# Weight sums in DRAM: copies issued by ScalarE, adds queued behind the decay rows, bias rows and last weights asked for earlier

## The chip, the cores and the metric

The kernel runs on one core of a Trainium2 chip. The core has five engines that run side by side, each through its own queue in order: TensorE (PE, matmuls; its weight loads are PEld), VectorE (DVE), ScalarE (ACT), GpSimd (POOL) and SyncE (SP). SP, ACT and POOL can issue DMAs, which 16 DMA engines carry out. The metric is the device time of one execution in microseconds. Before the change it is 1393.98 us, the median of three runs.

## What is computed

One decoder layer over 512 tokens of width 1024, in float32:

```
x = x + 0.5 * swiglu(rms_norm(x), ffn1_w_in, ffn1_w_out)          # D_FF = 2816
x = x + hybrid_mixer(rms_norm(x), ...)
x = x + memory_cross_attention(rms_norm(x), rms_norm(mem), ...)   # 256 memory tokens, 4 heads
x = x + 0.5 * swiglu(rms_norm(x), ffn2_w_in, ffn2_w_out)
return rms_norm(x)

# hybrid_mixer: one input projection, two groups of heads, one output projection
z, xbc, dt, q, k, v = split(h @ w_in)
y_ssd  = ssd_scan(conv(xbc), dt) * silu(z)      # 16 heads of 64, 4 groups, chunks of 128
#   decay = exp(la_cum[l] - la_cum[s]);  y = (c b^T * decay) xdt + carried state
y_attn = diff_attention(q, k, v, rel_bias)      # 8 heads, two softmaxes each
#   logits = q k^T / 8 + bias[bucket(k_pos - q_pos)]
return concat(y_ssd, y_attn) @ w_out
```

## The kernel before, in words

**Matmuls.** Each float32 weight tile is loaded to a buffer `wr` (six of them) and split into a high part `wh` by ScalarE (L151) and a low part `wl` by VectorE (L152), three buffers each. A product is three matmuls, high by high and the two mixed ones. `load_w` (L168) does load and split, `proj` (L296) a projection over eight tiles, 24 matmuls of 512 columns.

**Weight sums.** The last FFN multiplies in 2 by 2 blocks with seven products in place of eight (`quad`, L248, and `out_blocks`, L1107). Some of the seven take sums of weight blocks. These sums are made in DRAM while the mixer runs, by `block_sums_in_dram` (L1084): 46 jobs, each a copy of a block of 512 KB (a few of 256 KB) from the weights to `isum` or `wsum`, and an add, a DMA with accumulation of a second block onto it. Only POOL issues adds. Some add a sum that an earlier job made. The FFN's input sums are read by `quad`, its output sums by `out_blocks`; both start after the cross-attention.

**The order of the work.** The program is written as generators. `Order` (L53) runs them: the dense ones (projections) one after the other, and beside them chains (heads, groups, norms, the sums) that say after how many planned microseconds `od.t` they go on (`yield`). `od.t` counts matmul time alone. The instructions of SP stay in the order in which the program issues them; those of the other engines are set into their queues by a planner at build time, which may lift an instruction that it takes to be ready over an earlier one. `behind(ins)` (L180) forbids that against the instructions named: what is issued inside comes later in the same engine's queue. It adds an order, not a wait. `recent` holds the last weight tile's two split instructions. The list `hold` has an entry while a state-space group is between its start and its second set of decays; the sums then issue nothing.

**Attention heads.** `queries_keys(hd)` (L639) projects q, then k, and spawns `head(hd)` 3.4 planned us later. `head` first asks for the bias row of that head (L650, POOL, from the table `rel_z` in DRAM, 256 KB) and then makes scores (L653): a VectorE operation adds the bias and takes the minimum `mn` (L665), ScalarE takes exponentials, TensorE turns them (`turn`, tile `pt`).

**State-space groups.** `group(g)` (L779) runs four times. Its `decays(j)` (L785) asks POOL for two decay rows `r` (L790), 256 KB each, cumulated logs of one head broadcast to 128 partitions in pieces of 512 bytes. ScalarE makes exponentials of them (L849 to L852), VectorE multiplies by the masked products `cbm` (L853), and TensorE then makes `py` from them (L863). A group's norm uses POOL for a power (L335) and for one half of the row's diagonal (`ndiag`, L346).

**The end.** In `out_blocks` of the last third of the FFN, the product with `blocks[B22]` into `e_ps` is followed by `update` of two tiles, which calls `final`: squares on ScalarE, gain and scale on VectorE, a power on POOL (L1211), and two stores to the output by SP (L1213, L1215). Then follows the product with `sums[3]` into `b_ps`, whose weights are loaded by SP (L1117), and the last two updates with their stores.

Of the kernel before, what the change touches and what calls it, by code (L numbers as in the profile page):

```python
# [17 lines left out]
P = 128  # L18
# [11 lines left out]
RW = 640  # L30
NSLOT = 55
NHALF = 16

W = {"h0": 3.4, "hs": 3.3, "hv": 2.08, "hp": 6.75}
W |= {"g0": 8.28, "gc": 0.75, "gx": 0.92, "gb": 2.59, "gs": 0.51, "gd": 6.9, "gy": 0.38, "gq": 11.02, "gn": 6.52}
# [61 lines left out]
def body(tc, a, dbg=None):  # L97
# [13 lines left out]
    def nm(s):  # L111
        uid[0] += 1
        return f"{s}_{uid[0]}"
# [12 lines left out]
    def acc(s, shape=(P, T)):  # L126
        return acc_p.tile(list(shape), F32, tag="acc", name=nm(s))
# [5 lines left out]
        if dbg and name in dbg:  # L133
            nc.sync.dma_start(dbg[name], t.bitcast(F32) if t.dtype == R32 else t)

    last, start, last_sum, recent, hold = [], [], [], [], []
    V, S, G = nc.vector, nc.scalar, nc.gpsimd
    od = Order()

# [19 lines left out]
    def split(s, src, scale=None, half=False, n=T):  # L159
        if half:  # L160
            both = s2(s, R32, (P, 2, T // 2))
            hi, lo = both[:, 0], both[:, 1]
        else:
            hi, lo = s2(s + "h", R32, (P, n)), s2(s + "l", R32, (P, n))
        last[:] = [i.ins for i in split_into(hi, lo, src, scale)]
        return hi, lo
# [472 lines left out]
    def queries_keys(hd):  # L639
        pq = acc("pq")  # L640
        yield from proj(pq, load_w(a["wq"][hd]), h)
        q = split("q", pq, -1.0)
        pk = acc("pk")
        yield from proj(pk, load_w(a["wk"][hd]), h)
        kq = split("k", pk)
        od.spawn(head(hd, q, kq), W["h0"])

    def head(hd, q, kq):
        bias = s2("bias")
        nc.gpsimd.dma_start(bias, bass.AP(rel_z.tensor, rel_z.offset + hd * P * (RW + 1) + P - 1, [[RW, P], [1, T]]))  # L650
        es, w0, w1 = {}, {}, {}
        sm = [small("sm", 4) for _ in range(2)]

        def scores(i):
            n = P * (i + 1)
            ps = [aux("ps") for _ in range(2)]
            for j, (u, w) in enumerate(((0, 0), (0, 1), (1, 0))):
                for c in range(2):
                    pc = slice(64 * c, 64 * c + 64)
                    mm(ps[c][:, :n], q[u][pc, i * P : (i + 1) * P], kq[w][pc, :n], j == 0, j == 2)  # L660
            es[i] = []
            for c in range(2):
                ec = s2("ec", shape=(P, n))
                mn = small("mn", 1, bufs=8)
                V.tensor_tensor_reduce(out=ec[:, :n], in0=ps[c][:, :n], in1=bias[:, T - n :], scale=0.125, scalar=3e38, op0=ALU.add, op1=ALU.min, accum_out=mn)  # L665
                S.activation(ec[:, :n], ec[:, :n], AF.Exp, bias=mn, scale=-1.0, accum_out=sm[c][:, i : i + 1])  # L666
                es[i].append(ec)

        def combine(i):

            n = P * (i + 1)
            e = es[i]
            rc = small("rc", 1)
            V.reciprocal(rc, sm[1][:, i : i + 1])
            rl = small("rl", 1)
            V.scalar_tensor_tensor(rl, sm[0][:, i : i + 1], nlam, rc, ALU.mult, ALU.mult)
            V.scalar_tensor_tensor(e[0][:, :n], e[1][:, :n], rl, e[0][:, :n], ALU.mult, ALU.add)
            e.pop()

        def turn(j):  # L680
            n = P * (4 - j)
            pt = aux("pt")
            for i in range(j, 4):
                transpose(pt[:, (i - j) * P : (i - j + 1) * P], es[i][0][:, j * P : (j + 1) * P])
            if n <= T // 2:
                both = s2("wt", R32, (P, 2, n))
                w0[j], w1[j] = both[:, 0], both[:, 1]
            else:
                w0[j], w1[j] = s2("wt", R32, (P, n)), s2("wt", R32, (P, n))
            split_into(w0[j], w1[j], pt[:, :n])  # L690

        for s in range(6):
            if s < 4:
                scores(3 - s)
            if 1 <= s < 5:
                combine(4 - s)
            if s >= 2:
                turn(5 - s)
            yield W["hs"]
        es.clear()  # L700
        while hd // 4 not in vs:
            yield 1.0
        v = vs[hd // 4]
        hs = slice((hd % 4) * P, (hd % 4 + 1) * P)
        po = aux("po")
        for j in range(4):
            mm3(po[:, j * P :], v[j], (w0[j], w1[j]), j == 0, j == 3, wc=hs)
        w0.clear()
        w1.clear()
        of = s2("of")  # L710
        S.activation(of, po, AF.Copy)
        yield W["hv"]
        pt = aux("ptk")
        for b in range(4):
            transpose(pt[:, b * P : (b + 1) * P], of[:, b * P : (b + 1) * P])
        ss = small("ss", 4)
        junk = s2("junk", shape=(P, P))
        for b in range(4):
            S.activation(junk, pt[:, b * P : (b + 1) * P], AF.Square, accum_out=ss[:, b : b + 1])
        ev = small("ev", 4)  # L720
        V.scalar_tensor_tensor(ev, sm[0], EPS, sm[0], ALU.mult, ALU.mult)
        V.scalar_tensor_tensor(ev, ss, 1.0 / P, ev, ALU.mult, ALU.add)
        rr = small("rr", 4)
        G.tensor_tensor(rr, ev, mhalf, ALU.pow)
        on = s2("on", shape=(P, 4, P))
        V.tensor_tensor(on, pt.rearrange("p (a b) -> p a b", b=P), rr[:, :, None].to_broadcast([P, 4, P]), ALU.mult)
        yield W["hp"]
        pt = aux("pot")
        for b in range(4):
            transpose(pt[:, b * P : (b + 1) * P], on[:, b])  # L730
        ya[hd] = split("ya", pt, wsub)
        dump(f"ya_{hd}", ya[hd][0])
# [46 lines left out]
    def group(g, bt, ct, xs, zs):  # L779
# [5 lines left out]
        def decays(j):  # L785
            rs = []
            for hh in range(2):
                r = s2("r", shape=(P, 4, P))
                hd = 4 * g + 2 * j + hh
                nc.gpsimd.dma_start(r, bass.AP(cum_d.tensor, cum_d.offset + hd * P, [[0, P], [16 * P, 4], [1, P]]))  # L790
                rs.append(r)
            return rs

        hold.append(g)
# [289 lines left out]
    def block_sums_in_dram():  # L1084
        jobs = []
        for c, (f0, nf) in enumerate(THIRDS):
            gs = range(f0 // 2, (f0 + nf) // 2)
            jobs += [(isum[g][0], a["f2q"][g][0], a["f2q"][g][1]) for g in gs]
            jobs += [(isum[g][1], a["f2q"][g][2], isum[g][0]) for g in gs]
            blocks, sums = a[f"f2b{c}"], wsum[c]  # L1090
            for t, (to, more) in enumerate(((blocks[B12], blocks[B11]), (blocks[B12], blocks[B22]), (blocks[B22], sums[0]), (blocks[B21], sums[2]))):
                for k in range(0, nf // 2 * T, D):
                    ks = slice(k, min(k + D, nf // 2 * T))
                    jobs.append((sums[t][:, ks], to[:, ks], more[:, ks]))
        for n in range(len(jobs) + 2):
            while hold:
                yield 1.0
            if n < len(jobs):
                nc.sync.dma_start(jobs[n][0], jobs[n][1])
                yield 4.0  # L1100
            while hold:
                yield 1.0
            if n > 1:
                G.dma_start(jobs[n - 2][0], jobs[n - 2][2], accum_op=ALU.add, max_dma_last_dim=4 * D)
                yield 6.0

    def out_blocks(c, g, col4, last):  # L1107

# [2 lines left out]
        n = len(g)  # L1111
        parts = [(k, min(k + 2, n)) for k in range(0, n, 2)]

        def weights(of, part):
            w = (part[1] - part[0]) * T
            raw = wp.tile([P, w], F32, tag="wr", name=nm("wr"), bufs=6)
            nc.sync.dma_start(raw, of[:, part[0] * T : part[1] * T])  # L1117
            hi = wp.tile([P, w], R32, tag="wh", name=nm("wh"))
            lo = wp.tile([P, w], R32, tag="wl", name=nm("wl"))
            split_into(hi, lo, raw)  # L1120
            return hi, lo
# [8 lines left out]
                    nc.tensor.matmul(ps, a_[:, ts], b_[:, ws], start=first and k == 0 and j == 0, stop=k == n - 1 and j == 2, skip_group_check=True)  # L1130
                yield

        def product(ps, of, which, first=False, by_pair=False):
            if by_pair:
                ws = [weights(of, part) for part in parts]
                for t in range(2):
                    for w, part in zip(ws, parts):
                        yield from some(ps[t], w, which, part, t, first)
                return
            for part in parts:  # L1140
                w = weights(of, part)
                for t in range(2):
                    yield from some(ps[t], w, which, part, t, first)
# [36 lines left out]
        for t in range(2):  # L1180
            c22 = s2("c22")
            V.tensor_tensor(c22, p5[t], b_ps[t], ALU.subtract)
            update(t + 2, 1, c22)
        yield from product(e_ps, blocks[B22], S4)
        for t in range(2):
            update(t, 1, e_ps[t])
        yield from product(b_ps, sums[3], "22", by_pair=last is not None)
        for t in range(2):
            update(t + 2, 0, b_ps[t])

# [131 lines left out]
```

## Time and profile before

| What | Value |
|---|---|
| median of three runs | 1393.98 us (1392.22 to 1394.95) |
| the profiled execution: its own time, and its span | 1396.56 us, 1394.8 us |
| mean granted clock of TensorE | 0.98 |
| DMAs issued by SP: bytes, share of the DMA engines' time | 173.63 MB, 38.0% |
| DMAs issued by POOL | 47.79 MB, 20.7% |
| copies for sums: isum, wsum of 512 KB, issue to landing | 8.3 us, 5.5 us (medians) |
| adds for sums, issue to landing | 7.0 to 8.8 us (medians) |
| decay rows r; bias rows, issue to landing | 12.7 us; 6.0 us (medians) |

The profile is of one execution. Its span runs from the first to the last instruction; an engine is busy while it computes, and issuing a DMA isn't counted as busy for SP and ACT. A wait is put down to the instruction or DMA that ended it. A name such as `wsum<-in_f2b` gives what is written and what is read; L1104 is a line of the file. The granted clock is 1.00 at full speed; in this profile its records are either 1.0 or 0.5, so a mean between them says what part of a stretch ran at half speed. A time of "issue to landing" runs from the issuing instruction to the end of the transfer.

### The profile page before, as it was taken

The page shows a single profiled execution, that of the slowest core. Times are in us where ns is not written, and L with a number is a line of the kernel's source. Part 1 is how long each engine was busy: PE and PEld are TensorE (multiplying, and loading weights), DVE is VectorE, ACT ScalarE, POOL GpSimd, SP SyncE. Part 2 cuts the span into 40 slices and gives each one's busy share as a digit, 9 for nine tenths or more (in the row PEclk, how much of TensorE's full clock was granted, in tenths as well). Part 3 has the DMA queues.
Part 4 walks back from the last instruction along what each step waited for, and adds up shares of the span by engine and source line. Part 5 has one row for each costly group of instructions (what it writes and reads, how often), then busy time and mean ns, then how long its engine had stood idle before and what let it go on. Part 6 is the DMA issues. An engine that isn't in the chain of part 4 may idle for free.

```text
span 1394.8 us, 20038 instructions
## 1 busy us (share of the span) xinstructions
PE 1323.1 (95%) x7766; PEld 1146.3 (82%) x7766; DVE 977.0 (70%) x1533; ACT 668.7 (48%) x1124; POOL 134.4 (10%) x160
## 2 busy tenths in 40 slices
PE   8999999999999999989979995999999999999994
PEld 6888998899878687767868874888889989998983
DVE  6875777478875685547757874656687977887785
ACT  5442444245444554336544653434456554564563
POOL 1000010100221001211012031120000000000000
PEclk9999999999999999999999997999999999999997
DMA  7435576474898218973275678984136666666642
GB/s 258 117 111 121 148 204 214 106 191 142 260 265 217 69 39 162 283 201 78 60 164 140 91 182 172 249 205 113 61 91 173 174 190 189 170 183 189 182 139 83
DMA packets 65695, 222.71 MB, mean 160 GB/s; under 512 B 8424, under 2 KB 10960, under 8 KB 65248
## 3 DMA queue, kind: packets, MB, share of 16 engines
q1 hardware_dynamic: 51392, 173.63, 38.0%
q0 software_dynamic: 14208, 47.79, 20.7%
q8 instruction: 61, 1.00, 0.3%
q14 instruction: 34, 0.28, 0.1%
HBM read 219.24 MB, written 50.91 MB: 194 GB/s over the span
## 4 chain that ended last, share of the span: by engine, by line
PE 71%; DMA 10%; DVE 8%; issue 4%; ACT 3%; POOL 1%; SPq 0%; POOLq 0%; DVEq 0%; ACTq 0%
PE qb L231 10%; PE po L142 10%; PE qe L231 6%; PE pxbc L142 6%; PE pm L142 6%; PE qa L231 4%; DMA r<-cum_d 4%; PE ob L1130 3%; DVE wl L152 3%; PE pcq L142 3%; DMA wsum<-in_f2b 2%; PE pq L142 2%; PE oa L1130 2%; PE pz L142 2%; PE pk L142 2%
## 5 line engine op out<-in xcount | busy, mean ns | idle before, releaser
L151 ACT ACTIVATE wh<-wr 128x1024 fp32r<-128x1024 f32 (+2 forms) x311 | 316.5, 1021 | 373.6 <-issue 81.7
L152 DVE TENSOR_TENSOR wl<-wr,wh 128x1024 fp32r<-128x1024 f32 (+2 forms) x311 | 366.1, 1179 | 131.3 <-ACT wh L151 129.2
L142 PE MATMUL po<-gh,wh 128*128 128x512 f32 x176 | 68.8, 392 | 0.0
L142 PE MATMUL po<-gl,wh 128*128 128x512 f32 x176 | 68.5, 390 | 0.0
L142 PE MATMUL po<-gh,wl 128*128 128x512 f32 x176 | 68.4, 390 | 0.0
L231 PE MATMUL qa<-hmh,wl 128*128 128x256 f32 x216 | 61.2, 283 | 0.8 <-DVE wl L152 0.8
L231 PE MATMUL qa<-hml,wh 128*128 128x256 f32 x216 | 61.1, 283 | 0.0
L231 PE MATMUL qa<-hmh,wh 128*128 128x256 f32 x216 | 61.1, 283 | 0.0
L142 PE MATMUL pxbc<-hnh,wh 128*128 128x512 f32 x128 | 52.3, 408 | 0.0
L666 ACT ACTIVATE ec<-ec,mn 128x512 f32<-128x512 f32 (+3 forms) x64 | 35.4, 555 | 34.6 <-DVE mn L665 34.6
L142 PE MATMUL pxbc<-hnh,wl 128*128 128x512 f32 x128 | 50.3, 393 | 0.0
L142 PE MATMUL pxbc<-hnl,wh 128*128 128x512 f32 x128 | 50.2, 393 | 0.0
L231 PE MATMUL qb<-s31h,wh 128*128 128x256 f32 x152 | 43.9, 289 | 3.7 <-ACT u L277 3.7
L665 DVE CUSTOM_DVE_ANT_0 ec<-ps,bias 128x512 f32<-128x512 f32 (+3 forms) x64 | 28.8, 487 | 25.6 <-DMA bias<-rel_z 17.8
L231 PE MATMUL qe<-s31h,wh 128*128 128x256 f32 x152 | 44.0, 290 | 1.7 <-ACT wh L151 1.7
L231 PE MATMUL qe<-s31h,wl 128*128 128x256 f32 x152 | 43.8, 288 | 0.8 <-DVE wl L152 0.8
L231 PE MATMUL qb<-s24h,wh 128*128 128x256 f32 x152 | 43.2, 284 | 1.0 <-ACT qb L267 1.0
L231 PE MATMUL qe<-s31l,wh 128*128 128x256 f32 x152 | 43.7, 288 | 0.2 <-DVE s31l L152 0.2
L474 DVE TENSOR_TENSOR upd<-po,row 128x512 f32<-128x512 f32 x24 | 16.6, 691 | 38.1 <-PE po L142 38.0
L231 PE MATMUL qb<-s24h,wl 128*128 128x256 f32 x152 | 43.0, 283 | 0.0
L231 PE MATMUL qe<-s24h,wh 128*128 128x256 f32 x152 | 43.0, 283 | 0.0
L231 PE MATMUL qe<-s24l,wh 128*128 128x256 f32 x152 | 43.0, 283 | 0.0
(438 smaller groups left out, 4132.3 us busy)
## 6 DMA issues: line engine op xcount, KB each, us to landing
wr<-in_f2q SPq DMA_DIRECT2D x44, 512.0 KB, 4.3
wr<-in_f1q SPq DMA_DIRECT2D x40, 512.0 KB, 4.2
isum<-in_f2q SPq DMA_DIRECT2D x22, 512.0 KB, 8.3
wr<-isum SPq DMA_DIRECT2D x22, 512.0 KB, 4.1
wsum<-in_f2b SPq DMA_DIRECT2D x20, 512.0 KB, 5.5
wr<-wsum SPq DMA_DIRECT2D x20, 512.0 KB, 4.3
wr<-in_f1q POOLq DMA_DIRECT2D x16, 512.0 KB, 6.6
wr<-in_f1o SPq DMA_DIRECT2D x16, 512.0 KB, 4.5
```

The lines of the kernel that those rows point to most:

```text
L142: nc.tensor.matmul(out, w, x, start=start, stop=stop)
L151: S.activation(hi, src, AF.Copy),
L152: V.tensor_tensor(lo, src, hi.bitcast(F32), ALU.subtract),
L231: nc.tensor.matmul(out, a_[:, wc], b_, start=first and f == 0 and kp == 0 and j == 0, stop=kp == n - 1 and j == 2, skip_group_check=True)
L474: V.tensor_tensor(upd, po, row4, ALU.mult)
L665: V.tensor_tensor_reduce(out=ec[:, :n], in0=ps[c][:, :n], in1=bias[:, T - n :], scale=0.125, scalar=3e38, op0=ALU.add, op1=ALU.min, accum_ ...
L666: S.activation(ec[:, :n], ec[:, :n], AF.Exp, bias=mn, scale=-1.0, accum_out=sm[c][:, i : i + 1])
L1130: nc.tensor.matmul(ps, a_[:, ts], b_[:, ws], start=first and k == 0 and j == 0, stop=k == n - 1 and j == 2, skip_group_check=True)
```

## The change

Four parts. The copies of the sums are issued by ScalarE in place of SP, each placed behind the split of the last weight tile in ScalarE's queue, and the first check of `hold` in the loop, the one ahead of a copy, goes. An add follows its copy by four jobs in place of two, the round takes 9 planned us in place of 10, and each add stands behind the decay row that was issued last before it. The bias row is asked for between q's split and k's projection. And in the last third, the two loads of `sums[3]` are issued ahead of the updates of `e_ps`, that is, ahead of the stores.

```diff
+LEAD = 4
...
-    last, start, last_sum, recent, hold = [], [], [], [], []
+    last, start, last_sum, recent, hold, rows = [], [], [], [], [], []
...
         q = split("q", pq, -1.0)
+        bias = s2("bias")
+        nc.gpsimd.dma_start(bias, bass.AP(rel_z.tensor, rel_z.offset + hd * P * (RW + 1) + P - 1, [[RW, P], [1, T]]))
         pk = acc("pk")
         yield from proj(pk, load_w(a["wk"][hd]), h)
         kq = split("k", pk)
-        od.spawn(head(hd, q, kq), W["h0"])
+        od.spawn(head(hd, q, kq, bias), W["h0"])
 
-    def head(hd, q, kq):
-        bias = s2("bias")
-        nc.gpsimd.dma_start(bias, ...)
+    def head(hd, q, kq, bias):
...
-                nc.gpsimd.dma_start(r, bass.AP(cum_d.tensor, ...))
+                load = nc.gpsimd.dma_start(r, bass.AP(cum_d.tensor, ...))
                 rs.append(r)
+            rows[:] = [load.ins]
             return rs
...
-        for n in range(len(jobs) + 2):
-            while hold:
-                yield 1.0
+        for n in range(len(jobs) + LEAD):
             if n < len(jobs):
-                nc.sync.dma_start(jobs[n][0], jobs[n][1])
+                with behind([i for i in recent if i.engine == mybir.EngineType.Activation]):
+                    S.dma_start(jobs[n][0], jobs[n][1])
                 yield 4.0
             while hold:
                 yield 1.0
-            if n > 1:
-                G.dma_start(jobs[n - 2][0], jobs[n - 2][2], accum_op=ALU.add, max_dma_last_dim=4 * D)
-                yield 6.0
+            if n >= LEAD:
+                to, _, more = jobs[n - LEAD]
+                with behind(rows):
+                    G.dma_start(to, more, accum_op=ALU.add, max_dma_last_dim=4 * D)
+                yield 5.0
...
-        def weights(of, part):
-            w = (part[1] - part[0]) * T
-            raw = wp.tile([P, w], F32, tag="wr", name=nm("wr"), bufs=6)
+        def fetch(of, part):
+            raw = wp.tile([P, (part[1] - part[0]) * T], F32, tag="wr", name=nm("wr"), bufs=6)
             nc.sync.dma_start(raw, of[:, part[0] * T : part[1] * T])
+            return raw
+
+        def weights(of, part, raw=None):
+            raw = raw or fetch(of, part)
+            w = raw.shape[1]
...
-        def product(ps, of, which, first=False, by_pair=False):
-            if by_pair:
-                ws = [weights(of, part) for part in parts]
+        def product(ps, of, which, first=False, raws=None):
+            if raws:
+                ws = [weights(of, part, raw) for part, raw in zip(parts, raws)]
...
         yield from product(e_ps, blocks[B22], S4)
+        raws = last and [fetch(sums[3], part) for part in parts]
         for t in range(2):
             update(t, 1, e_ps[t])
-        yield from product(b_ps, sums[3], "22", by_pair=last is not None)
+        yield from product(b_ps, sums[3], "22", raws=raws)
```

## What was predicted

> **What bounds the kernel now.** I began with the page: span, busy engines and shares of the chain that ended last.
>
> ```profile
> span 1394.8 us, 20038 instructions
> ...
> PE 1323.1 (95%) x7766; PEld 1146.3 (82%) x7766; DVE 977.0 (70%) x1533; ACT 668.7 (48%) x1124; POOL 134.4 (10%) x160
> ...
> PE 71%; DMA 10%; DVE 8%; issue 4%; ACT 3%; POOL 1%; SPq 0%; POOLq 0%; DVEq 0%; ACTq 0%
> ```
>
> TensorE is busy for 1323.1 of 1394.8 us, so no edit that leaves the matmuls alone can win more than its idle time and what the lowered clock adds to it. DMA has 10% of the chain: somewhere TensorE's work waits for transfers. So the next view is who waited for whom, first for PE (columns: us in total, times, longest), then for POOL.
>
> ```profile
> PE py L142 <- DVE r L853: 28.6, 7, 15.7
> PE ob L1130 <- ACT wh L151: 11.6, 1, 11.6
> PE pt L146 <- DVE mn L665: 5.4, 2, 2.7
> ...
> PE nrow L142 <- POOL ndiag L346: 2.1, 2, 1.7
> ```
> ```profile
> POOL wsum L1104 <- DMA wsum<-in_f2b: 220.5, 24, 27.1
> POOL isum L1104 <- DMA isum<-in_f2q: 147.0, 19, 45.7
> ```
>
> Four places hold most of PE's waits: the state product py, which needs the decay rows r; the last product ob; the scores, whose minimum mn needs the bias; a norm row, which needs POOL. And POOL stood 367 us (220.5 + 147.0) in front of adds whose copy had not landed. Whatever stands behind such an add in POOL's queue came late with it. The table of stretches prices each place (columns: stretch, length, busy PE, PEld, DVE, ACT, POOL, then granted clock, DMA share, GB/s); the last three rows start where PE had restarted.
>
> ```profile
> 462.00:469.00 7.00, 4.36 (x14) 3.35 (x13) 5.90 (x19) 4.61 (x14) 0.00 (x0) 0.76 0.23 71
> 546.00:565.00 19.00, 14.79 (x80) 11.53 (x80) 14.11 (x23) 10.88 (x24) 1.72 (x2) 0.91 0.86 244
> 582.00:585.00 3.00, 1.25 (x6) 0.73 (x5) 0.32 (x1) 0.00 (x0) 1.93 (x2) 1.00 1.06 365
> 614.00:626.00 12.00, 7.61 (x28) 5.17 (x26) 9.54 (x26) 6.00 (x16) 1.39 (x2) 0.72 0.47 117
> 720.00:732.00 12.00, 4.98 (x27) 3.79 (x26) 7.03 (x10) 9.61 (x23) 0.00 (x0) 0.72 0.70 161
> 830.00:862.00 32.00, 14.51 (x75) 10.53 (x74) 11.32 (x17) 14.53 (x29) 3.43 (x4) 0.73 0.74 136
> 1368.00:1384.00 16.00, 4.41 (x12) 2.79 (x11) 6.77 (x14) 5.00 (x10) 1.62 (x2) 0.68 0.35 115
> 620.00:626.00 6.00, 6.00 (x19) 4.38 (x19) 4.91 (x15) 3.97 (x11) 0.00 (x0) 0.51 0.13 51
> 857.00:862.00 5.00, 5.00 (x22) 3.57 (x23) 2.98 (x5) 5.00 (x9) 0.00 (x0) 0.55 0.58 107
> 1380.00:1384.00 4.00, 3.68 (x8) 2.53 (x9) 1.83 (x2) 0.75 (x2) 0.00 (x0) 0.54 0.00 0
> ```
>
> A stretch loses its length less PE's busy time, and then one less the clock, times the length at which matmuls ran slow. A (462:469, bias): 2.64 idle + 0.24 x 7 = 4.3. B (546, decay rows of group 0): 4.21 + 0.09 x 19 = 5.9. C (582, norm row): 1.75. D (614, bias): 4.39 + 0.49 x 6 = 7.3. E (720, group 1): 7.02, and of 0.28 x 12 = 3.4 I take 2.1, the part past the restart: 9.1. F (830, group 3): 17.49 + 0.45 x 5 = 19.7. G (1368, the last product): 11.59 + some 1.7 of 0.46 x 4 = 13.3. **A to F hold 48.1 us, with G 61.4.** That is the ceiling of what these edits can reach.
>
> **The change part by part.** POOL's and SP's queues in order of time, for A, D, E, group 2 (which has no stall) and F; the bracket is the idle time before it and what ended it.
>
> ```profile
> 453.05 0.81 POOL L1104 DMA_DIRECT2D wsum<-wsum  x1 [7.82 <-DMA wsum<-in_f2b]
> 453.58 1.43 POOL L650 DMA_DIRECT2D bias<-rel_z  x2
> ...
> 605.62 0.81 POOL L1104 DMA_DIRECT2D isum<-isum  x1 [3.51 <-DMA isum<-in_f2q]
> ...
> 708.22 0.89 POOL L1104 DMA_DIRECT2D wsum<-in_f2b  x1 [11.81 <-DMA wsum<-in_f2b]
> 708.85 3.34 POOL L790 DMA_DIRECT2D r<-cum_d  x4
> ...
> 765.37 1.62 POOL L790 DMA_DIRECT2D r<-cum_d  x2 [7.81 <-DVE th L751]
> ...
> 834.85 0.93 POOL L1104 DMA_DIRECT2D wsum<-wsum  x1 [17.03 <-DMA wsum<-in_f2b]
> 835.46 1.91 POOL L790 DMA_DIRECT2D r<-cum_d  x2
> ```
> ```profile
> 712.82 4.94 SPq L1099 DMA_DIRECT2D wsum<-in_f2b  x1
> ...
> 824.72 2.54 SPq L1099 DMA_DIRECT2D wsum<-in_f2b  x1
> ```
>
> In A, E and F the load goes out right behind an add that had waited 7.8 to 17 us for its copy (in D the next bias follows the add of 605.62, which had waited 3.5); F's copy had only been issued by SP at 824.72, and took 2.54 us to issue. Group 2's rows had no add before them and PE shows no stall there. *Copies on ScalarE, adds four jobs behind:* at 4 + 5 us of planned work a job, an add comes some 36 us behind its copy; the slowest copy landed in 19.8 us (median 6.6, row below), so adds stop waiting. *Adds behind the rows:* F's add was hoisted over loads that the program issues first; the new order forbids it. The adds wait for nothing new but the loads' places; behind them stand biases, rows and norms, which are no worse off. Who waits for sums is the last FFN, from 1001 us on; 50 rounds of 9 us of planned work end no later than 48 of 10 do now, so that costs nothing.
>
> ```profile
> DMA to landing us min/median/max: 3.7/6.6/19.8
> ```
> ```profile
> DMA to landing us min/median/max: 8.3/12.7/23.8
> ```
> ```profile
> 1001.52 1.90 SPq L237 DMA_DIRECT2D wr<-isum  x2
> ```
>
> (The first row is the copies', the second the decay rows' r.) What each place yields: **A, D:** bias waits go, since it is asked for ahead of the 24 matmuls of pk and stands behind no stuck add: 4.3 + 7.3. **C:** POOL's half of the norm row stands in the same queue; bound 0 to 1.75, I take 1.75. **E:** rows could go up to 11.81 us sooner, the stall is 7.0: all 9.1. **B:** bound 0 to 5.9; whether the rows had a buffer any sooner the trace doesn't show; I take 3. **F:** the second pair could go up to 17 us sooner, but then its transfer meets the first pair's, and a load takes 8.3 us at best: bound 0 to 19.7, I take 15.7, about half of those 8.3 less, as group 2 is the nearest row. Middle: 41.2.
>
> **G:** SP's queue and VectorE's at the end:
>
> ```profile
> 1350.85 1.27 SPq L1117 DMA_DIRECT2D wr<-in_f2b  x2
> 1372.61 0.34 SPq L1213 DMA_DIRECT2D out<-x  x1
> ...
> 1374.48 1.24 SPq L1117 DMA_DIRECT2D wr<-wsum  x2
> ```
> ```profile
> 1371.98 1.03 DVE L1214 TENSOR_SCALAR x<-x,frr 128x512 f32<-128x512 f32 x2
> ...
> 1384.44 0.75 DVE L1146 SCALAR_TENSOR_TENSOR x<-ob,col,x 128x512 f32<-128x512 f32 x1 [2.35 <-PE ob L1130]
> ```
>
> The last weights stand behind four stores that wait for the normed rows. Asked for ahead, they follow the pair of 1350.85 as soon as buffers come free, well before PE needs them near 1369; the stores then stand behind two issues of 0.6 us and lose nothing. Late next is VectorE: it ends the earlier tiles' rows at 1373.0, now with the last lower halves (1.83 us in the stretch 1380:1384) among them, so the first update of ob starts near 1374.8 instead of 1384.44, and all behind it moves along: 9.6. Bounds: 11.4 with the halves hidden; 6 where the planner leaves both splits behind the rows.
>
> **What it costs.** SP loses 46 issues (rows below, 24 + 22 at a median of 0.50: 23 us), ScalarE gains them. ScalarE is busy 246.9 of 520 us there, so most is hidden; if that cover were gone, all 23 us. I take 3, by its share of the chain. Below nothing isn't excluded: SP's loads now go 0.5 us sooner behind each copy; 0 for that.
>
> ```profile
> L1099 SPq DMA_DIRECT2D wsum<-in_f2b x24: 490/502/4937, 400.3 to 963.3; - x24
> L1099 SPq DMA_DIRECT2D isum<-in_f2q x22: 499/499/1155, 349.5 to 890.5; - x22
> ```
> ```profile
> 400.00:920.00 520.00, 481.89 (x2398) 384.74 (x2397) 329.25 (x657) 246.90 (x535) 72.95 (x86) 0.96 0.64 157
> ```
>
> The bias holds one of 55 buffers some 9 us longer (pk's 24 matmuls and 3.4 us of lead); 0, bounded by group 2's wait for a buffer, 7.8 us, which stalled nobody.
>
> **Sum:** 4.3 + 3 + 1.75 + 7.3 + 9.1 + 15.7 + 9.6 - 3 = 47.8. The profiled execution took 1396.56 us, 1.8 over its span and 2.6 over the median of 1393.98; the stalls are of the program's order, so I take the gain off the median: 1346.2.
>
> **Rivals.** *All of it comes out:* 61.4 less nothing, 1333. Against it: r's own transfers, 12.7 us in the median, and VectorE's work at the end.
>
> *The transfers are what is slow.* The slowest row landed 23.8 us after its issue, and at B the DMA engines were 0.86 busy. If the rows land as late as now, B, E and F stay, and A, C, D, G give 23: 1371. Against it: group 2, with the same rows, no add before them and no stall. The Trainium skill says under "DMA: Bandwidth & Descriptors", in "Issuing engines are not separate DMA queues", that DMAs from any engine end on the same 16 DMA engines, and that issuing from several saves the issue time alone. By that rule, moving the copies would free SP of 23 us that bind nobody, and this rival's time would follow; the trace disagrees in one point: the copies bind through POOL's queue (367 us of waiting), and no run here shows yet what freeing it does to a row's transfer.
>
> *ScalarE held at the issue: slower.* With rows in flight SP's issue of one copy took 4.94 us (712.82) instead of 0.50. ScalarE works in order: behind a stuck copy stand the weights' upper halves and the exponentials of those same rows. At 4.94 us for each, 46 copies hold it 227 us, with its 247 busy nearly all of the 520; if a third of it reached PE, 76 us against 50.8: 1419. It decides at about 1.1 us a copy reaching PE. Against it: the median issue is 0.50, and by the loop at most one copy goes out while a group holds the adds.
>
> *It doesn't do what it says:* the planner leaves adds ahead of rows and splits behind stores' rows, and all stays within 0.2% (about what a measurement of this kernel can tell from no change): 1394.
>
> **Chances.** Forecast 0.54, all 0.14 (1333), transfers 0.20 (1371), unchanged 0.04, slower 0.08. The range 1331 to 1372 takes in the first three and leaves out what lies beyond them. Faster 0.88, same 0.04, slower 0.08.
>
> **What would show it.** POOL's waits for wsum and isum copies fall from 367 us to under 50; no add stands right before an r or bias; PE's wait for r (28.6) falls under 8 and for ob (11.6) under 2; the clock at 830 to 862 is over 0.9; the last weights' load stands ahead of the first store. Wrong: rows landing later than 24 us, new PE waits for wh in 400 to 920, copies on ScalarE over 2 us each.

## The result, and the profile after

| | before | after |
|---|---|---|
| median, same job | 1394.47 us | 1356.76 us (1351.76 to 1361.01) |
| ratio, 95% interval | | 0.9708 [0.9636, 0.9781] |
| span of the profiled execution | 1394.8 us | 1357.1 us |
| mean granted clock | 0.98 | 0.988 |

The change made the kernel faster by 37.7 us, between the forecast of 47.8 us and the rival of 23. The page of after, span, busy engines and shares of the chain:

```profile
span 1357.1 us, 20038 instructions
...
PE 1318.0 (97%) x7766; PEld 1143.3 (84%) x7766; DVE 978.6 (72%) x1533; ACT 668.4 (49%) x1124; POOL 134.3 (10%) x160
...
PE 80%; DVE 7%; DMA 4%; issue 3%; ACT 3%; POOL 1%; POOLq 0%; DVEq 0%; ACTq 0%
```

DMA fell from 10% of the chain to 4%. TensorE's work is the same 7766 matmuls; what went is idle time and time at half clock. After's view of waits, for PE (us in total, times, longest):

```profile
PE pn L144 <- POOL ysq L885: 6.4, 1, 6.4
PE py L144 <- DVE r L856: 5.1, 3, 1.8
...
PE ps L144 <- DVE mn L667: 2.8, 1, 2.8
```

The waits for decay rows fell from 28.6 to 5.1, and that for the last product (11.6) is gone. But the first line is new: the norm of a group waits 6.4 us for a square that POOL makes. And POOL's own waits did not fall to the "under 50" that I had named:

```profile
POOL isum L1108 <- DMA isum<-in_f2q: 98.2, 14, 23.1
POOL wsum L1108 <- DMA wsum<-in_f2b: 86.9, 12, 14.2
POOL wsum L1108 <- DMA wsum<-wsum: 21.5, 2, 18.5
```

Those are 207 us of 367. Where each part of the time went can be told from when TensorE starts the same product in both profiled executions (its first matmul of a value projection `pv`, of each group's `pcb`, of the cross-attention's queries, of the last FFN, and of its last third). Differences between these starts, in us:

| stretch | places in it | before | after | gain | forecast |
|---|---|---|---|---|---|
| up to the first pv | | 406.9 | 406.7 | 0.2 | 0 |
| to group 0 | A | 121.8 | 121.4 | 0.4 | 4.3 |
| to group 1 | B, C, D | 174.4 | 159.2 | 15.2 | 12.05 |
| to group 2 | E | 65.2 | 55.9 | 9.3 | 9.1 |
| to group 3 | (group 2) | 41.0 | 47.8 | -6.8 | 0 |
| to the cross-attention | F | 105.6 | 98.6 | 7.0 | 15.7 |
| to the last third | | 428.0 | 427.3 | 0.7 | 0 |
| to the end | G | 51.9 | 40.2 | 11.6 | 9.6 |
| ScalarE's issues | | | | 0 | -3 |

So B, C, D, E and G came at their size or better, and three rows did not: A, F, and group 2, which had no stall before. The table of stretches of after for those three (stretch, length, busy PE, PEld, DVE, ACT, POOL, granted clock, DMA share, GB/s):

```profile
415.00:428.00 13.00, 10.20 (x47) 7.96 (x46) 10.04 (x45) 5.92 (x20) 0.80 (x1) 0.87 0.84 191
769.00:780.00 11.00, 7.48 (x31) 5.67 (x30) 6.66 (x9) 5.53 (x12) 0.00 (x0) 0.69 0.65 213
822.00:848.00 26.00, 17.72 (x74) 13.33 (x74) 14.26 (x22) 12.44 (x22) 5.58 (x5) 0.80 0.96 278
840.70:847.50 6.80, 6.77 (x20) 5.71 (x21) 3.65 (x7) 2.21 (x3) 2.99 (x3) 0.50 0.87 299
```

The last row starts where PE had restarted. Read as in the prediction, the first stretch lost 2.80 + 0.13 x 13 = 4.5 us and the second some 3.52 + 0.5 x 6.1 = 6.6 (PE restarted at 773.2 and ran at half clock up to 779.3). The third lost 8.28 + 0.5 x 6.8 = 11.7. The first two are new; the third holds the 1.6 us that are left of F's wait for rows, and the new wait of 6.4 us for the square. Where that comes from is seen in after's POOL queue in order of time, and then in ScalarE's:

```profile
796.27 1.52 POOL L792 DMA_DIRECT2D r<-cum_d  x2
...
798.31 1.49 POOL L792 DMA_DIRECT2D r<-cum_d  x2
799.79 1.82 POOL L1108 DMA_DIRECT2D wsum<-wsum  x2
800.95 1.50 POOL L1108 DMA_DIRECT2D isum<-in_f2q  x1
805.68 0.81 POOL L1108 DMA_DIRECT2D isum<-in_f2q  x1 [3.22 <-DMA r<-cum_d]
810.82 0.81 POOL L1108 DMA_DIRECT2D isum<-in_f2q  x1 [4.33 <-DMA r<-cum_d]
834.77 0.81 POOL L1108 DMA_DIRECT2D isum<-isum  x1 [23.14 <-DMA isum<-in_f2q]
838.89 1.78 POOL L885 TENSOR_TENSOR ysq<-ysq,ysq 128x512 f32<-128x512 f32 x1 [3.31 <-ACT ysq L883]
```

```profile
833.40 1.06 ACT L153 ACTIVATE wh<-wr 128x1024 fp32r<-128x1024 f32 x1 [2.21 <-DMA wr<-in_wos]
837.23 1.06 ACT L153 ACTIVATE wh<-wr 128x1024 fp32r<-128x1024 f32 x1 [2.78 <-DMA wr<-in_wos]
...
838.20 0.61 ACT L883 ACTIVATE ysq<-y 128x512 f32<-128x512 f32 x1
```

The rows go first, as the change wants. But five adds follow in one bunch, and the next, at 834.77, adds a sum that one of the five makes, so it waited 23.14 us for that one to land, with the group's square behind it in the queue. That wait was not the last to end, though. POOL then stood another 3.31 us for the second of the two squares that it adds up, which ScalarE makes. VectorE had the input of that one ready at 832.5 (its product at 831.84 took 0.68 us), but in ScalarE's queue it stood behind two splits of weight tiles, and these waited for their loads. The six loads that SP issued from 801.2 to 820.5 landed after 22.3 to 25.4 us. The same six took 8.2 to 18.2 us in the run without the order, and 7.2 to 18.9 us in the run without adds (both below). So the bunch of adds delays the weights, and through them the square. The adds of `isum` issued in 799 to 840, after:

```profile
L1108 POOL DMA_DIRECT2D isum<-in_f2q x3: 812/814/1502, 801.0 to 810.8; - x3
...
DMA to landing us min/median/max: 12.2/32.4/33.3
```

An add took 6.8 to 8.4 us in the same part of the kernel before. In a bunch behind four decay rows it takes four times as long, and so it did behind the rows of group 1 (three adds at 682.39 to 683.55: 27.5 to 34.9 us).

### The profile page after: what moved, and what is told of

Same layout as the page of the kernel before. It is cut to its first block, busy times and chain, and to the rows that moved or that the text cites. A ratio compares the mean times of both kernels' runs of the same rounds, so it can differ in the third digit from the quotient of the medians.

```text
span 1357.1 us, 20038 instructions
## 1 busy us (share of the span) xinstructions
PE 1318.0 (97%) x7766; PEld 1143.3 (84%) x7766; DVE 978.6 (72%) x1533; ACT 668.4 (49%) x1124; POOL 134.3 (10%) x160
## 4 chain that ended last, share of the span: by engine, by line
PE 80%; DVE 7%; DMA 4%; issue 3%; ACT 3%; POOL 1%; POOLq 0%; DVEq 0%; ACTq 0%
PE qb L233 11%; PE po L144 10%; PE pm L144 10%; PE qe L233 7%; PE pxbc L144 5%; PE qa L233 4%; PE pz L144 3%; PE pcq L144 3%; PE ob L1138 3%; PE pk L144 3%; PE pq L144 3%; PE pv L144 3%; PE oa L1138 2%; DVE wl L154 2%; PE oe L1138 2%
## 5 line engine op out<-in xcount | busy, mean ns | idle before, releaser
L233 PE MATMUL qe<-s24h,wl 128*128 128x256 f32 x152 | 43.0, 283 | 0.0
```

The lines of the kernel that those rows point to most:

```text
L233: nc.tensor.matmul(out, a_[:, wc], b_, start=first and f == 0 and kp == 0 and j == 0, stop=kp == n - 1 and j == 2, skip_group_check=True)
```

## The experiments

Times are medians; each ratio is against runs of the kernel before on the same chip (medians of 1395.6 to 1396.5 us there), with its 95% interval. "As after, but" and "as before, but" name the base of each.

**The tail alone** (as before, but the last weights ahead of the stores):

```diff
+        raws = last and [fetch(sums[3], part) for part in parts]
         for t in range(2):
             update(t, 1, e_ps[t])
-        yield from product(b_ps, sums[3], "22", by_pair=last is not None)
+        yield from product(b_ps, sums[3], "22", raws=raws)
```

> Edit: the kernel before with the last weights asked for ahead of the stores, and nothing else. My theory: the wait of ob (11.6 us) goes and the end of the kernel comes 9.6 to 12 us sooner, 1382 to 1385 us; the waits for decay rows and bias stay as they were (PE waits some 28 us for r). Rival (the planner leaves the weights' splits behind the output rows): 6 us, 1388. Rival (VectorE's updates only move the wait): under 2 us.

1382.02 us, 0.9895 [0.9864, 0.9926], a gain of 14 by the medians and 12.1 on the spans (1394.8 to 1382.7). G stands by itself.

**The bias alone** (as before, but the bias row asked for with the keys):

```diff
         q = split("q", pq, -1.0)
+        bias = s2("bias")
+        nc.gpsimd.dma_start(bias, ...)
...
-    def head(hd, q, kq):
-        bias = s2("bias")
-        nc.gpsimd.dma_start(bias, ...)
+    def head(hd, q, kq, bias):
```

> The kernel before with one part of the change alone: the bias row of a head asked for with its keys. Theory (terms A and D of the forecast's sum, 4.3 and 7.3 us, of which A was given back by a new bias wait in head 0): 1383 to 1391 us, with the waits at 462 and 614 gone. Rival (the bias row then stands behind the adds' waits for copies of the kernel before, on the same engine): 1393 to 1400 us, the bias waits moved and not gone.

1385.44 us, 0.991 [0.9874, 0.9946]. The places A and D in this run's stretches:

```profile
462.00:469.00 7.00, 7.00 (x40) 5.09 (x39) 5.84 (x19) 3.96 (x12) 0.55 (x1) 1.00 0.35 109
605.00:626.00 21.00, 21.00 (x116) 15.54 (x115) 17.66 (x54) 12.80 (x35) 2.85 (x4) 1.00 0.70 180
```

PE is busy throughout at full clock. The stretch to group 0 fell from 121.8 to 116.7 us (5.1; forecast for A 4.3), that to group 1 from 174.4 to 167.2 (7.2; forecast for D 7.3). Both terms are there when nothing else is changed.

**The bias late** (as after, but the bias asked for in `head`, as before the change; the diff is the last one turned round).

> Edit: the changed kernel with the bias asked for in the head as before. Theory (bias waits came from stuck adds ahead of it in POOL's queue, not from being asked late): within 4 us of the changed kernel, 1353 to 1361 us. Rival (asking earlier is what removed places A and D): PE waits 4 us or more for mn and the time is 8 to 12 us longer, 1365 to 1369 us.

1375.86 us, 0.9848 [0.9806, 0.9889], 19 us over after: the rival was right and too small. The wait is for the first head's minimum, and POOL's queue shows why:

```profile
PE pdk L144 <- DVE mn L667: 7.3, 1, 7.3
```

```profile
396.46 0.81 POOL L1108 DMA_DIRECT2D isum<-isum  x1 [3.28 <-DMA isum<-in_f2q]
...
409.48 2.93 POOL L603 TENSOR_TENSOR ea<-euler,hb 128x16 f32<-128x16 f32 x1 [11.07 <-DMA hb<-in_hb]
...
413.00 0.90 POOL L652 DMA_DIRECT2D bias<-rel_z  x1
```

The adds go up to 396.46, the load of `hb` follows them, POOL waits 11.07 us for it, and the bias goes out behind that at 413.00; before the change it went at 394.55. The early bias is worth 11 us alone and 19 with the rest of the change.

**Copies on ScalarE alone** (as before, but `S.dma_start` behind the last split for the copy; lead of two and both checks of `hold` kept).

> The kernel before with one part of the change alone: the copies of the weight sums issued by ScalarE; adds and biases stay where they were. Theory (who issues the copy decides how long POOL's adds hold the rows and norms behind them; terms B, C and E of the sum, 16.8 us, and part of F): 1367 to 1382 us. Rival (the adds, not the copies, are what lands late; rows stay late behind them): 1388 to 1398 us.

1387.54 us, 0.9921 [0.989, 0.9952]: between the two, just short of the rival's 1388, and neither mechanism alone. Group 0 to 2 gained (174.4 to 162.5 and 65.2 to 55.7 us), but the heads before group 0 lost 11.3 us (121.8 to 133.1). POOL's queue in this run, and the wait that it made:

```profile
466.93 0.85 POOL L1105 DMA_DIRECT2D wsum<-in_f2b  x1 [8.04 <-DMA wsum<-in_f2b]
473.39 0.82 POOL L1105 DMA_DIRECT2D wsum<-in_f2b  x1 [5.62 <-DMA wsum<-in_f2b]
473.94 0.86 POOL L650 DMA_DIRECT2D bias<-rel_z  x1
```

```profile
PE ps L142 <- DVE mn L665: 8.1, 3, 5.7
```

Who issues the copies and when the bias is asked for belong together: the first without the second moves adds in front of biases. F gained only 3.1 us here (105.6 to 102.5): an add at 829.79 had waited 19.30 us for its copy, with the second pair of rows behind it. The dropped first check of `hold` was not tried by itself, so its share in F's gain is not shown.

**Copies on SP** (as after, but the copy by SP), and **the same without the order behind the rows**:

```diff
-                with behind([i for i in recent if i.engine == mybir.EngineType.Activation]):
-                    S.dma_start(jobs[n][0], jobs[n][1])
+                nc.sync.dma_start(jobs[n][0], jobs[n][1])
```

> Edit: the changed kernel with the copies issued by SP as before, the lead of four jobs, the order behind rows and the rest kept. Theory (lead and order do it; who issues the copy hardly matters): within 5 us of the changed kernel, 1352 to 1362 us. Rival (SP's queue was what made copies late; adds wait for them again): POOL's waits for copies go back over 250 us in all and the time to 1366 to 1380 us.

1382.42 us, 0.991 [0.9879, 0.994], longer than both theories had it. POOL's waits were 196 us, less than after's 207, and yet PE waits more:

```profile
PE pn L144 <- POOL ysq L885: 19.1, 2, 10.5
PE py L144 <- DVE r L856: 9.9, 4, 6.1
PE nrow L144 <- DVE ndiag L348: 5.1, 2, 4.6
```

> The changed kernel with the copies issued by SP again (as before the change) and without the order of the adds behind the decay rows. [...] Rival (the order behind the rows was what made SP's copies harmful): within 6 us of the run without the order, 1345 to 1357 us.

I had put 1370 to 1385 us on copies that stand in SP's queue and land late. 1364.78 us, 0.9768 [0.9724, 0.9811], lies between that and the rival: 14 us slower than with ScalarE's copies and no order (the next run). The stall that is left is one of 9.4 us, and it can be followed through three queues, SP's first, then POOL's, then PE's wait:

```profile
780.03 20.00 SPq L172 DMA_DIRECT2D wr<-in_wcv  x4
800.08 0.49 SPq L1100 DMA_DIRECT2D isum<-in_f2q  x1
```

```profile
804.98 0.91 POOL L1106 DMA_DIRECT2D isum<-isum  x1 [8.52 <-DMA isum<-in_f2q]
...
808.27 1.87 POOL L792 DMA_DIRECT2D r<-cum_d  x2
```

```profile
PE py L144 <- DVE r L856: 13.3, 3, 9.4
```

SP's four weight loads stretch over 20.00 us (a row with a count runs from the first start to the last end). Each landed after 3.5 to 3.8 us; SP's waits in 770 to 800 are put down to VectorE's split `wl`, the last reader of a `wr` buffer (six waits, up to 9.6 us). The copy behind them left at 800.08; the add had waited 8.52 us when it landed; the decay rows stood behind the add.

**No order behind the rows** (as after, but):

```diff
-                with behind(rows):
-                    G.dma_start(to, more, accum_op=ALU.add, max_dma_last_dim=4 * D)
+                G.dma_start(to, more, accum_op=ALU.add, max_dma_last_dim=4 * D)
```

> Edit: the changed kernel without the order of adds behind decay rows. Theory (a copy's lateness was the harm, four jobs of lead are enough): no add waits long for its copy, so an add ahead of rows costs its 1 us of issue, and without the bunch of adds behind the rows the 6.4 us wait of pn for POOL's ysq goes: 1345 to 1352 us. Rival (the order is what keeps the rows early): adds stand ahead of rows again, PE waits 10 us or more for r, 1366 to 1380 us.

1350.64 us, 0.9667 [0.9636, 0.9698]: the span is 1345.5 against after's 1357.1. The intervals overlap, so that it is faster than after rests on the stall that went. This run's PE wait, and POOL's queue behind the rows of 794.89 to 798:

```profile
PE pn L144 <- POOL ysq L885: 1.3, 1, 1.3
```

```profile
821.39 0.94 POOL L1107 DMA_DIRECT2D isum<-isum  x1 [22.96 <-PE pcv L144]
830.43 1.78 POOL L885 TENSOR_TENSOR ysq<-ysq,ysq 128x512 f32<-128x512 f32 x1 [8.11 <-ACT ysq L883]
```

No add goes out beside these rows; the planner had put two at 770 and 774 and the next at 821, and the adds of `isum` then landed in 7.6 to 9.0 us. The square is no longer late; it waits for ScalarE's half here too, which is there sooner. F's stretch took 88.4 us, 17.2 less than before the change. The four combinations, medians in us:

| | adds behind the rows | no such order |
|---|---|---|
| copies on SP | 1382.4 | 1364.8 |
| copies on ScalarE | 1356.8 | 1350.6 |

ScalarE's copies are worth 14 to 26 us, and the order costs 6 to 18 (the 6 is the difference whose intervals overlap).

**Adds held until the norm's row** (as after, but `hold` ends with the group, and the adds stand behind POOL's half of the norm's diagonal in place of the decay row):

```diff
-            eng.tensor_tensor(diag, ...)
+            made = eng.tensor_tensor(diag, ...)
+        rows[:] = [made.ins]
...
-            if j == 1:
-                hold.remove(g)
...
+        hold.remove(g)
```

> Edit: the changed kernel with the adds held until a group's norm row is made, and placed behind POOL's last instruction of that norm (the order behind decay rows kept). Theory (the new wait is the group's square sum behind a stuck add): pn's 6.4 us wait and half clock go, and rows land sooner with no adds beside them: 1342 to 1350 us. Rival (the adds, pushed together after the groups, collide with the cross-attention or the last FFN): 1355 us or more.

1345.22 us, 0.964 [0.9613, 0.9668]. No wait for r or for the norm's square is left; PE's waits of over 1 us in the mixer are two for a bias, of 2.8 us in head 0 and of 2.6 at 606. So it is not order as such that costs, but an order that releases the adds between a row and the norm.

**No adds at all** (as after; the copies stay, the 46 adds are left out, so the last FFN reads unfinished sums).

> Edit: the changed kernel with all 46 adds left out (the copies stay, so the last FFN works with weight blocks instead of their sums; the work left out is POOL's queue entries and the adds' transfers alone). Theory (what is left of the stalls in the mixer comes from adds bunched behind the decay rows): the waits at 420 (2.8 us), 769 (3.5), 822 (1.6) and 834 (6.4) go, with the half clock behind them some 20 us: 1334 to 1342 us. Rival (they come from the rows' own transfers and from buffers): within 8 us of the changed kernel, 1349 to 1360.

1341.45 us, 0.9609 [0.9578, 0.964]. Of after's stalls in the mixer those at 420, 771 and 834 are gone, and PE waits 1.4 us for rows and 1.3 for the square: after's losses are the adds' doing, and the copies alone make next to none.

**Each copy in two halves** (as after; 92 issues on ScalarE).

> Edit: the changed kernel with every copy issued by ScalarE in two halves, 92 issues in place of 46, the same bytes. This doubles the cost of issuing on ScalarE. Theory (the cost is hidden): within 4 us of the changed kernel, 1353 to 1361 us. Rival (my term of 3 us, or more of the 23 us of issue time): 3 to 23 us longer, 1360 to 1380.

1364.2 us, 0.9778 [0.9747, 0.9809], 7.4 over after, which looks like the rival; but by the starts of the products the loss (7.3 us) lies ahead of group 0, where the first bias came late, and no later stretch is longer by more than 0.4 us. Doubling the issues cost nothing where ScalarE works most. The first bias went out at 414.83, behind `ea`, which waited 13.20 us for the load of `hb`, much as in the run with the late bias; in after it goes ahead of `ea`, at 397.67. Why the planner set it behind with halves is open.

**The sums begun later** (as without the order, but the chain of sums starts 50 planned us after its place, not 10), and **a lead of two** in that version:

```diff
-            od.spawn(block_sums_in_dram(), 10.0)
+            od.spawn(block_sums_in_dram(), 50.0)
```

> Edit: e2 (no order behind decay rows) with the sums begun 50 planned us after the first FFN in place of 10, so that the first adds don't stand ahead of the first head's bias. Theory (head 0's bias landed late because it was issued beside five adds and loads): the 2.8 us wait at 419 and its 1.7 us of half clock go: 4 us under e2, 1343 to 1349 us. Rival (the same crowding moves to the next head or group): within 2 us of e2 or longer.

1339.8 us (1339.16 to 1342.11), 0.9607 [0.9575, 0.9639]: the fastest version, below both kernels, and as fast as the one with no adds. The same three stretches as above:

```profile
415.00:428.00 13.00, 12.75 (x64) 10.03 (x63) 8.58 (x35) 4.89 (x15) 2.23 (x3) 1.00 0.71 202
769.00:780.00 11.00, 11.00 (x55) 9.21 (x54) 8.00 (x14) 4.03 (x7) 3.19 (x4) 1.00 0.73 182
822.00:848.00 26.00, 25.32 (x107) 20.56 (x108) 16.13 (x25) 9.95 (x14) 5.25 (x6) 0.93 0.82 230
```

POOL's waits for copies in it are as long as before the change:

```profile
POOL wsum L1107 <- DMA wsum<-in_f2b: 219.4, 21, 35.5
...
POOL isum L1107 <- DMA isum<-in_f2q: 142.9, 20, 20.7
```

> The fastest version so far (the change without the order behind the rows, the sums begun earlier; 1339.8 us) with a copy two jobs ahead of its adds in place of four. Theory (POOL's waits for copies of 365 us did no harm there, so the lead is not what the gain hangs on): 1337 to 1343 us. Rival (a shorter lead lengthens the waits of the adds in front of rows and biases): 1345 us or more, with a stall of PE at a group boundary that the version with four lacks.

(The sums of that version begin later, not earlier.) 1340.89 us, 0.9602 [0.9559, 0.9645]: no difference that this can tell. One stall of 2.2 us for a row at 813 is new. In this version the longer lead is not where the gain comes from.

## Why the prediction was right, and where its size was off

**What bounds the kernel: right.** The ceiling of 61.4 us was the right order: the best version gains 57.4 us on the span, and by the same starts it has the terms nearly as forecast, each measured against its own: A 3.9 (4.3), B with C and D 15.3 (12.05), E 8.7 (9.1), F 15.6 (15.7), G 11.7 (9.6).

**A: the mechanism right, the gain given back.** The bias wait at 462 is gone, and alone it was worth 5.1. In the change the first head's bias went out at 397.67, behind adds and two other loads in POOL's queue, and VectorE waited 5.65 us for it:

```profile
395.99 0.81 POOL L1108 DMA_DIRECT2D isum<-isum  x1 [2.49 <-DMA isum<-in_f2q]
...
397.67 0.81 POOL L646 DMA_DIRECT2D bias<-rel_z  x1
```

```profile
410.71 0.69 DVE L667 CUSTOM_DVE_ANT_0 ec<-ps,bias 128x512 f32<-128x512 f32 x1 [5.65 <-DMA bias<-rel_z]
```

**B, C, D, E: right.** B had been put at 3 between 0 and 5.9; the three together measured 15.2, and the upper end for B would make 14.95. E measured 9.3 for 9.1.

**Group 2 and F: the step that failed.** It is the sentence "The adds wait for nothing new but the loads' places; behind them stand biases, rows and norms, which are no worse off". It put the adds' own transfers at nothing. Adds that are held for rows come out in a bunch right behind them. Behind group 3's rows they landed after 27 to 33 us in place of 7 to 9, and the weight loads issued meanwhile after 22 to 25 us in place of 8 to 18; ScalarE's splits waited for these loads, with a square of the norm behind them. The other way to the norm, by POOL's queue, is open too: a chained add waits for one of the bunch, with the square behind it. In after that wait ended 3.31 us too early to matter, but with the copies on SP it was the last: ScalarE had its half done by 846.3, and POOL began at 855.74, right behind an add of 855.19. F's own wait for rows did go, from 15.7 us to 1.6, and 6.4 us of idle and 6.8 us of matmuls at half clock took its place. Without the order F measured 17.2 in place of 7.0.

Group 2's loss of 6.8 is of a second kind: its fourth row (752.82) landed after 14.6 us, with two adds right behind it (754.41). But without the order the loss stays (47.5 us for that stretch) and the row took 14.1 us, though no add was in flight beside it: the last one had landed at 738.0, and the next went out at 770.33. The loss is gone with the norm-held adds (41.0 us, the row 10.7), and for the most part without adds (42.5, 12.1) and with the sums begun later (41.8, 10.3). So the loss follows how late this row lands; what makes the row late is not shown.

**G: right, its size 2 us low.** The first update of `ob` starts at 1348.41, 31.5 us after the last third begins, against 41.5 before: 10.0 for 9.6. The other 1.6 us are behind it: before, the second update followed 3.2 us after the first, behind VectorE's work on the first tile's rows, and now 0.66 us after it.

```profile
1347.46 1.03 DVE L1223 TENSOR_SCALAR x<-x,frr 128x512 f32<-128x512 f32 x2
1348.41 1.40 DVE L1154 SCALAR_TENSOR_TENSOR x<-ob,col,x 128x512 f32<-128x512 f32 x2
```

**ScalarE's 3 us: not there.** Its 46 issues took 0.50 us each, and no PE wait for `wh` appeared in 400 to 920:

```profile
L1101 ACTq DMA_DIRECT2D wsum<-in_f2b x24: 497/498/498, 427.9 to 924.6; - x24
```

The slower rival needed 1.1 us of each copy to reach PE.

**The reason that I gave for the gain was half wrong.** "Adds stop waiting", by the lead of four, was the claim, and 367 us to under 50 its test. The waits fell to 207, and the best version has 365. What counts is what stands behind a waiting add. In the best version the lead added nothing; ScalarE's queue, where a copy does not stand behind the weight loads, and the early bias did. Other signs that I had named spoke against it too: an add still stands right before four of the eight biases (459.16, 583.07, 601.88, 616.78), the clock behind group 3 was 0.80 (822 to 848) and not over 0.9, and one row, issued at 681.65, landed after 24.5 us, where over 24 was to mean that I was wrong. The four combinations above speak against the Trainium skill's rule ("DMA: Bandwidth & Descriptors", "Issuing engines are not separate DMA queues") as the rival of 1371 had used it: by it the issuer matters for its issue time alone, and here the same copies are 14 to 26 us dearer on SP. By the queues shown above, what is saved is not 46 times 0.50 us but the place behind loads that stretch over 20.00 us in SP's queue. The rule's other half, that the transfers interleave on the same DMA engines, agrees with this trace: beside the adds that POOL issued, SP's weight loads took 22 to 25 us in place of 8 to 18.

In sum: of 47.8 forecast, A lost 3.9, group 2 6.8 and F 8.7; B to D gave 3.15 more, E 0.2, G 2.0, ScalarE 3 and the rest 0.9; 37.6 on the spans.

**Left open.** Why an add lands late behind the rows is shown in part. In every trace here POOL's DMAs landed in the order of their issue: in after the four rows at 805.4, 810.5, 815.0 and 820.5, then the five adds at 826.7, 830.5, 834.3, 838.1 and 843.2. A bunch alone does part of it: in the norm-held run five adds with no row in flight (884.59 to 886.78) landed after 6.4, 11.2, 15.3, 19.5 and 21.4 us. Why the rows themselves take so long was only argued: in after's stretch 799 to 812 the DMA engines are 0.95 busy at 127 GB/s, and in the run without the order, with the same rows and no add, 0.97 at 150. The rows, in pieces of 512 bytes, seem to fill the engines without moving much. Rows in larger pieces were not tried.

## What to carry to other kernels

An engine's total waiting says little; look at which instruction stands behind each wait in the same queue, and move either the wait or that instruction, for the best version here waits as long as the first. When a wait is put down to an engine, look what that engine was itself waiting for: here PE waited for POOL, POOL for ScalarE, and ScalarE for weights. Before tying work behind something ("after the rows"), ask what it will then collide with and what comes next in the queue: held work is released in a bunch, and a bunch of transfers lands late and delays the loads beside it. Try each part of a change alone and left out: here two parts that needed each other (ScalarE's copies, early bias) hid one that cost time (the order).

## What the runs showed of the hardware that I had not expected

- POOL's DMAs landed in the order of their issue in all fourteen traces. Accumulating DMAs that land in 7 to 9 us alone took 27 to 33 us in a bunch of five behind four decay rows of 256 KB in pieces of 512 bytes (after, 799 to 811), and 6.4 to 21.4 us in a bunch of five with no rows (norm-held adds, 885 to 887). Weight loads that SP issued beside the first bunch took 22 to 25 us, against 8 to 18 without it.
- An idle stretch of 2.80 us on TensorE (after, 420.2) was followed by 3.4 us of half clock, which cost 1.7 us on top. Behind the idle 6.4 us at 834 the matmuls ran at half clock for 6.8 us, which cost 3.4 us on top.
- ScalarE issued each copy in 0.50 us among its activations. No wait of TensorE is put down to these issues with 46 of them, and with 92 no stretch behind group 0 was longer by more than 0.4 us.
